# Ranking weight loads and splits ahead of their place in the recording, with new load durations, in a two-layer decoder trunk on one core

## The chip, the cores and the metric

The kernel runs on one core of one Trainium2 chip. Times are device microseconds (us) of one execution. TensorE is PE in the profile, VectorE is DVE, ScalarE is ACT, GpSimd is POOL, and SyncE is SP, whose queue issues the DMAs. PE's weight loads are a row of their own, PEld. TensorE's clock has two levels, 1.2 and 2.4 GHz; the profile gives the granted clock as a share of full speed (PEclk).

## The reference, cut to what matters

The input is one sequence of 512 tokens with 1024 features, and there are two layers (`DEPTH = 2`), each two half-step FFNs around a mixer with two branches:

```python
for l in range(DEPTH):
    x = x + 0.5 * swiglu(rmsnorm(x, ffn1_norm[l]), ffn1_w_gate_up[l], ffn1_w_down[l])
    h = rmsnorm(x, mix_norm[l])
    (q, kc, vc, ksel, vsel, kwin, vwin, g_nsa, uv, g_a, g_b) = \
        jnp.split(h @ w_in[l], IN_SPLITS, axis=-1)
    ...
    y_a = nsa_attention(...)
    y_b = spatial_gating(uv, sgu_norm[l], sgu_w_s[l], sgu_b_s[l])
    merged = jax.nn.sigmoid(g_a) * (y_a @ proj_a[l]) + jax.nn.sigmoid(g_b) * (y_b @ proj_b[l])
    x = x + merged @ w_out[l]
    x = x + 0.5 * swiglu(rmsnorm(x, ffn2_norm[l]), ffn2_w_gate_up[l], ffn2_w_down[l])
return rmsnorm(x, final_norm)
```

In `nsa_attention` the keys and values `kc` and `vc` are compressed: 31 overlapping windows of 32 tokens, plus a position term, go through a small network (`gelu(flat @ w1) @ w2`, called phi below). `spatial_gating` is `u * (tril(W_s) v + b)` on `gelu(uv)`, with `v` normalised. All weights are float32.

## The kernel before, in words

**Recording and ordering.** The kernel does not issue instructions as it runs. Every call on an engine goes through `Recorder.note`, which keeps the operation with the earlier operations it depends on, a rank, and a planned duration. The rank is the operation's index in the recording plus a bias of its engine (no bias is set for the engines here); the duration comes from `Recorder.cost`, as a pair: how long the engine is busy, and after how long the result can be used. `Recorder.order` is a list scheduler: again and again it takes the engine that can start earliest and, among the operations of that engine that are ready by then, the one with the lowest rank. `issue` emits the operations in the order found, so each engine, and SP's queue with its DMAs, runs them strictly in that order. All of them carry one line in the profile (L255, and L259 in the changed file).

**Weight tiles.** Nearly all the work of PE is 128-row tiles of weights against 512 tokens. `load` fetches one tile: SP copies 128x1024 float32 (512 KB) into `raw` (3 buffers), ACT copies it to `whi` (3 buffers, in the matmul format fp32r), and DVE computes `wlo = raw - whi` (2 buffers). The activations are split the same way, into `xh` and `xl` (`split`, `norm_operand`). `chain` then issues three matmuls for each of eight 128-row pieces: high by high, high by low, and low by high, 24 matmuls a tile. As `wlo` has two buffers, the subtraction for tile n overwrites what PE reads for tile n-2, and has to wait for it.

**The course of a layer.** `ffn` runs 44 gate and up tiles and three groups of eight down tiles. `mix` is the mixer. Its first part, in the order of recording:

- *Stage A:* projections of `kc` and `vc`; `windows` turns each into four tiles R18 to R21 (keys) or R14 to R17 (values): for each half of the partitions two DVE products (`t<-b,rbc`), one DVE sum (`t<-t,pes`) and a split into `R` on ACT and DVE. Then `proj_tok` with the weights wv (four banks b4 to b7), whose four steps are interleaved with the four of `phi` for keys (matmuls `b<-whi,R` and `b<-wlo,R`).
- *Stage B:* the gelu of that result into `YA`, a norm on it (`rsqrt`, then `YA<-YA,rv,ga` and the split into `VH` and `VL`, four each), while PE runs the `u` half (wu) and phi for values.
- *Stage C:* keys and queries with rotary tables (`roped`: ACT copies, DVE and POOL products, `R` splits and casts), the spatial gating (matmuls `b<-VH,whi`, then `U<-b,sgub,U`), transposes of `U` (`b<-cst,U`), and the first tiles of the gates (wB).

Then attention, the projections of both branches and wo follow, and the second `ffn`.

The program's first loads, before any matmul, are the gains, the eight pieces of `x`, and the first two weight tiles, on SP in turn; `norm_begin` and `norm_prep` make `xh`, `xl` and the squares of the norm.

Of the kernel before, what the change touches and what calls it, by code (L numbers as in the profile page):

```python
# [22 lines left out]
NG = (3 * DEPTH + 1) * KD  # L23
CHUNKS = ((0, 8), (8, 16), (16, 22))
LAG = 1
NEG = -1e30
EPS = 1e-6

# [10 lines left out]
class View:  # L39


    def __init__(self, buf, steps, ids, parts, dtype):
        self.buf, self.steps, self.ids, self.parts, self.dtype = buf, steps, ids, parts, dtype
        self.gen = buf.gen
# [88 lines left out]

class Recorder:
    def __init__(self, nc):
        self.nc, self.ops, self.rings, self.bias = nc, [], {}, {}
        self.real = {"PE": nc.tensor, "DVE": nc.vector, "ACT": nc.scalar, "POOL": nc.gpsimd, "SP": nc.sync}

    def ring(self, tag, n, cols, dtype=F32, psum=False):
# [19 lines left out]
    def note(self, engine, op, args, kw):  # L159
        outs = [v for v in [args[0], kw.get("accum_out")] if isinstance(v, View)]  # L160
        ins = [v for v in list(args[1:]) + [v for k, v in kw.items() if k != "accum_out"] if isinstance(v, View)]
        i, deps = len(self.ops), set()
        for v, writes in [(v, False) for v in ins] + [(v, True) for v in outs]:
            assert v.gen == v.buf.gen, v.buf.name
            q, e = v.region()
            keep = []
            for j, jw, jq, je in v.buf.log:
                if (writes or jw) and jq & q and je & e:
                    if j != i:
                        deps.add(j)  # L170
                    if writes and jq & ~q == 0 and je & ~e == 0:
                        continue
                keep.append((j, jw, jq, je))
            keep.append((i, writes, q, e))
            v.buf.log = keep
        self.ops.append((engine, op, args, kw, deps, i + self.bias.get(engine, 0), self.cost(engine, op, args, kw, outs, ins)))

    def cost(self, engine, op, args, kw, outs, ins):

        if engine == "PE":  # L180
            n = outs[0].ids.size
            if op == "transpose":
                return 109, 280
            rhs = kw["rhs"]
            if rhs.dtype == F32:
                t = 2 * max(109, n / 1.2 + 3)
                return t, t + 165
            t = max(109, n / 2.4 + 13.3)
            return t, t + 165
        if engine == "SP":  # L190
            v = outs[0] if outs else ins[0]
            size = (v.parts[1] - v.parts[0]) * v.ids.size * 4
            return 100 + size / 190, 2000 + size / 330
        a, b = SBUF_COST[engine]
        n = max(v.ids.size for v in outs + ins)
        if engine == "DVE" and op in ("tensor_copy", "tensor_scalar") and not any(v.buf.psum for v in ins):
            b = 0.52
        if op == "memset":
            b = b / 2
        t = a + b * n  # L200
        if kw.get("accum_out") is not None:
            t += 190 if engine == "ACT" else 83
        return t, t

    def order(self):
        ops = self.ops
        users, left = [[] for _ in ops], [len(o[4]) for o in ops]
        for i, o in enumerate(ops):
            for j in o[4]:
                users[j].append(i)  # L210
        ready = [0.0] * len(ops)
        free = dict.fromkeys(self.real, 0.0)
        cand = {e: [] for e in self.real}
        table, out = 0, []
        for i, o in enumerate(ops):
            if not left[i]:
                cand[o[0]].append(i)
        while len(out) < len(ops):
            best = None
            for e, c in cand.items():  # L220
                if not c:
                    continue
                t = max(free[e], min(ready[i] for i in c))
                if best is None or t < best[0]:
                    best = t, e
            t, e = best
            i = min((i for i in cand[e] if ready[i] <= t), key=lambda i: ops[i][5])
            cand[e].remove(i)
            busy, lat = ops[i][6]
            if e == "ACT":  # L230
                f = next((a for a in list(ops[i][2]) + list(ops[i][3].values()) if a in TABLES), None) \
                    if ops[i][1] == "activation" else None
                if f is not None and TABLES[f] != table:
                    table, busy, lat = TABLES[f], busy + 1283, lat + 1283
            free[e] = t + busy
            out.append(i)
            for u in users[i]:
                same = ops[u][0] == e
                ready[u] = max(ready[u], t + (busy if same and e != "SP" else lat + 70))
                left[u] -= 1  # L240
                if not left[u]:
                    cand[ops[u][0]].append(u)
        self.span = max(free.values())
        return out
# [14 lines left out]
def trunk(ctx: ExitStack, tc, d):  # L259
    rec = Recorder(tc.nc)  # L260
# [41 lines left out]
    def f(ap):  # L302
        return ap.bitcast(F32)

    def split(hi, lo, src):

        act(hi, src, AF.Copy)
        vec.tensor_tensor(lo, src, f(hi), op=ALU.subtract)
# [3 lines left out]
    def stage(src, n, mask=None):  # L312
        if first:
            return first.pop(0)
        return load(src, n, mask)

    def load(src, n, mask=None):
        raw, hi, lo = (rec.tile(t, [P, 1024]) for t in ("raw", "whi", "wlo"))
        sync.dma_start(raw[:, :n], src)
        if mask is not None:  # L320
            mask(raw)
        split(hi[:, :n], lo[:, :n], raw[:, :n])
        return hi, lo

    def mm3(ps, lh, ll, rh, rl, start, stop):
# [7 lines left out]
    def chain(ps, ops):  # L333

        n = len(ops)
        for k in range(n + LAG):
            if k < n:
                lh, _, rh, rl = ops[k]
                pe.matmul(ps, lhsT=lh, rhs=rh, start=k == 0, stop=False)
                pe.matmul(ps, lhsT=lh, rhs=rl, start=False, stop=False)  # L340
            if k >= LAG:
                _, ll, rh, _ = ops[k - LAG]
                pe.matmul(ps, lhsT=ll, rhs=rh, start=False, stop=k == n + LAG - 1)

# [601 lines left out]
    for k in range(KD):  # L946
        sync.dma_start(x[:, k, :], d["x"][k])
        if k < 2:
            first.append(load(d["gu1"][0, k], 1024))
# [16 lines left out]
def layout(inp):  # L966
# [60 lines left out]
    c[:, C_TRI:C_TRI + P] = r[:, None] <= r[None, :]  # L1027
    c[:, C_MASK + 384:C_MASK + 512] = np.where(r[None, :] <= r[:, None], 0.0, NEG)
    c[:, C_CM:C_CM + 56] = np.where(16 * (np.arange(56)[None, :] - 24) + 31 <= r[:, None], 0.0, NEG)
    c[:, C_VAL] = r >= 31  # L1030
# [24 lines left out]
```

## Time and profile before

| | |
|---|---|
| median of 3 runs | 2235.32 us (2233.21 to 2235.88) |
| the profiled execution | 2233.7 us, span of its instructions 2231.9 us |
| mean granted TensorE clock | 0.991 |
| busy: PE, PEld | 2187.2 us (98%), 1808.3 us (81%) |
| busy: DVE, ACT, POOL | 1158.8 us (52%), 889.9 us (40%), 258.4 us (12%) |
| DMA | 207.3 MB by SP's queue, mean 94 GB/s |
| a 512 KB load of gate/up weights | 3.5 us from issue to landing (median of 176) |
| all waits of PE: on DVE `wlo`, ACT `whi`, DVE `U`, DVE `VL` | 15.5, 11.1, 6.7, 2.5 us |

The profile is one execution. The busy time of an engine counts from the start to the modelled end of its instructions, and matmuls overlap, so a matmul's own duration is longer than its distance to the next. "Waits" are times in which an engine had nothing running, put down to what released it. A "window" is a stretch of the span with the busy time of each engine in it, and the granted clock averaged over it. PE waits for nothing from 30 to 370 us or from 600 to 1480 us: its waits lie in the first 24 us, in the first part of the mixer of each layer (stages A to C), and in the last 11 us.

### The profile page before, as it was taken

How to read it: one execution, taken by the hardware profiler on the slowest of the kernel's cores; microseconds unless marked ns; L12 is line 12 of the kernel's file. 1: busy time of each engine (PE TensorE's matmuls, PEld its weight loads, DVE VectorE, ACT ScalarE, POOL GpSimd, SP SyncE). 2: the span in 40 equal slices, each digit the busy share in tenths (PEclk: the TensorE clock that was granted, in tenths of full speed). 3: DMA queues.
4: the chain of work that ended last, by engine and by line, in shares of the span. 5: the costliest groups of instructions: out<-in, count | busy, mean ns of one | idle time of the engine just before them, and what ended most of it. 6: DMA issues, size and time to landing. Idle time of an engine off the chain costs nothing. (4 is left out here: it accounts for less than half of the span.)

```text
span 2231.9 us, 25665 instructions
## 1 busy us (share of the span) xinstructions
PE 2187.2 (98%) x10018; PEld 1808.3 (81%) x10018; DVE 1158.8 (52%) x1884; ACT 889.9 (40%) x1414; POOL 258.4 (12%) x165
## 2 busy tenths in 40 slices
PE   8999999889999999999999999999999999999998
PEld 6888888678888888888888888877788888888887
DVE  5334346568886433333543333374788855333334
ACT  5223234466663432322432232345666534323233
POOL 2102012010000120111211020110100001101011
PEclk9999999999999999999999999999999999999999
DMA  4323323322113233333333223234211233323322
GB/s 166 103 95 95 98 94 93 118 90 73 55 60 100 99 96 101 97 95 95 95 102 100 95 95 100 87 98 136 78 57 57 62 107 91 99 95 95 101 93 80
DMA packets 61033, 208.95 MB, mean 94 GB/s; under 512 B 7280, under 2 KB 7792, under 8 KB 60912
## 3 DMA queue, kind: packets, MB, share of 16 engines
q1 hardware_dynamic: 60912, 207.32, 29.6%
q8 instruction: 78, 1.28, 0.2%
q14 instruction: 43, 0.35, 0.0%
HBM read 205.19 MB, written 2.10 MB: 93 GB/s over the span
## 5 line engine op out<-in xcount | busy, mean ns | idle before, releaser
L255 ACT ACTIVATE whi<-raw 128x1024 fp32r<-128x1024 f32 (+2 forms) x396 | 409.0, 1036 | 904.1 <-PE b L255 855.5
L255 PE MATMUL b<-xh,whi 128*128 128x512 f32 x1920 | 754.0, 393 | 9.6 <-ACT whi L255 9.5
L255 PE MATMUL b<-xl,whi 128*128 128x512 f32 x1920 | 753.2, 392 | 0.3 <-DVE xl L255 0.3
L255 PE MATMUL b<-xh,wlo 128*128 128x512 f32 x1920 | 717.6, 393 | 1.6 <-DVE wlo L255 1.5
L255 DVE TENSOR_TENSOR wlo<-raw,whi 128x1024 fp32r<-128x1024 f32 (+2 forms) x396 | 471.2, 1191 | 88.8 <-PE b L255 56.6
L255 PEld LDWEIGHTS b<-xh,whi 128*128 128x128 f32 x1920 | 362.0, 189 | 86.5 <-ACT whi L255 11.5
L255 PEld LDWEIGHTS b<-xh,wlo 128*128 128x128 f32 x1920 | 361.6, 188 | 78.1 <-DVE wlo L255 3.6
L255 PEld LDWEIGHTS b<-xl,whi 128*128 128x128 f32 x1920 | 362.0, 189 | 76.0 <-DVE xl L255 1.7
L255 PE MATMUL b<-R,whi 128*128 128x512 f32 (+1 forms) x1428 | 420.1, 387 | 0.0
L255 DVE TENSOR_TENSOR t<-b,rbc 128x512 f32<-128x512 f32 (+1 forms) x192 | 132.4, 690 | 404.0 <-PE b L255 403.4
L255 POOL TENSOR_TENSOR t<-t,t 128x512 f32<-128x512 f32 x88 | 184.4, 2095 | 1153.0 <-DVE t L255 1143.2
L255 PEld LDWEIGHTS b<-R,whi 128*128 128x128 f32 x1428 | 267.1, 188 | 55.4
L255 PE MATMUL b<-R,wlo 128*128 128x512 f32 (+1 forms) x714 | 260.4, 387 | 0.0
L255 DVE SCALAR_TENSOR_TENSOR x<-b,x 128x512 f32<-128x512 f32 (+1 forms) x113 | 77.7, 687 | 296.4 <-PE b L255 296.4
L255 ACT ACTIVATE R<-t 128x512 fp32r<-128x512 f32 (+3 forms) x152 | 81.4, 551 | 242.2 <-POOL t L255 214.0
L255 DVE TENSOR_TENSOR R<-t,R 128x512 fp32r<-128x512 f32 (+3 forms) x152 | 91.7, 616 | 164.1 <-ACT R L255 163.5
L255 PEld LDWEIGHTS b<-R,wlo 128*128 128x128 f32 x714 | 134.0, 188 | 26.9
L255 PE MATMUL b<-R,R 128*128 128x512 f32 (+3 forms) x416 | 116.5, 358 | 0.2
L255 POOL TENSOR_TENSOR ga<-ga,t 128x512 f32<-128x512 f32 x35 | 48.7, 1391 | 419.5 <-ACT t L255 419.3
L255 PEld LDWEIGHTS b<-R,R 128*128 128x128 f32 x416 | 74.3, 189 | 13.0 <-DVE R L255 0.6
L255 ACT ACTIVATE R<-b 128x512 fp32r<-128x512 f32 (+1 forms) x84 | 48.3, 580 | 79.1 <-PE b L255 74.7
L255 PE MATMUL b<-wlo,xh 128*128 128x512 f32 (+1 forms) x192 | 72.4, 378 | 1.3 <-DVE wlo L255 1.3
(132 smaller groups left out, 1605.0 us busy)
## 6 DMA issues: line engine op xcount, KB each, us to landing
raw<-in_gu_dram SPq DMA_DIRECT2D x176, 512.0 KB, 3.5
raw<-in_dn_dram SPq DMA_DIRECT2D x64, 512.0 KB, 3.5
raw<-in_wA_dram SPq DMA_DIRECT2D x48, 512.0 KB, 3.5
raw<-in_dn_dram SPq DMA_DIRECT2D x32, 384.0 KB, 3.1
raw<-in_phi_dram SPq DMA_DIRECT2D x16, 512.0 KB, 4.0
raw<-in_wo_dram SPq DMA_DIRECT2D x16, 512.0 KB, 3.6
raw<-in_wv_dram SPq DMA_DIRECT2D x8, 512.0 KB, 3.8
raw<-in_wu_dram SPq DMA_DIRECT2D x8, 512.0 KB, 3.7
```

The source lines that it names most:

```text
L255: getattr(self.real[engine], op)(*args, **kw)
```

## The change

Two things change, both in the recorder. First, while `load` records its DMA, a mask if there is one, and the two operations of its split, their rank is lowered by `AHEAD = 100`, so that among ready operations of an engine they are taken before any other whose index is up to 100 lower. Second, the planned time of a DMA is new. Before, a transfer of `size` bytes kept SP busy for 100 + size/190 ns and was usable after 2000 + size/330 ns, each by itself (2859 and 3589 ns for 512 KB). Now it keeps SP busy for 430 ns, and the data of all transfers go through one pipe one after another, at 400 bytes per ns, after 2000 ns each (1311 ns of pipe for 512 KB).

```diff
+AHEAD = 100
...
-        self.nc, self.ops, self.rings, self.bias = nc, [], {}, {}
+        self.nc, self.ops, self.rings, self.bias, self.ahead = nc, [], {}, {}, 0
...
-        self.ops.append((engine, op, args, kw, deps, i + self.bias.get(engine, 0), self.cost(engine, op, args, kw, outs, ins)))
+        self.ops.append((engine, op, args, kw, deps, i + self.bias.get(engine, 0) - self.ahead, self.cost(engine, op, args, kw, outs, ins)))
...
-            return 100 + size / 190, 2000 + size / 330
+            return 430, size / 400
...
-        table, out = 0, []
+        table, out, dma = 0, [], 0.0
...
+            if e == "SP":
+                dma = max(dma, t + 2000) + lat
+                lat = dma - t
...
+        rec.ahead = AHEAD
         sync.dma_start(raw[:, :n], src)
         if mask is not None:
             mask(raw)
         split(hi[:, :n], lo[:, :n], raw[:, :n])
+        rec.ahead = 0
```

Every engine issues the same operations as before. POOL's order does not change. On SP little moves: at the start the loads of the first two weight tiles go ahead of the gains and all of `x`, and at the mixer's start the load of `pes` goes behind two further weight loads. ACT, DVE and PE change order in some hundreds of places, nearly all in the mixer; in the FFNs a `wlo` changes places with one neighbour. Three places follow, all on DVE in layer 1 (layer 2 has them too).

**Stage A, the windows of keys and values.** Names: `t` are scratch tiles, b0 and b1 the projections, R18 to R21 the keys' windows and R14 to R17 the values'. Before, the end of that run of operations:

```order
L255 TENSOR_TENSOR t_0_77<-b1_0_164,rbc_0_69 64x496
L255 TENSOR_TENSOR t_1_78<-t_0_77,pes_0_65 128x496
L255 TENSOR_TENSOR wlo_1_116<-raw_2_76,whi_2_114 128x1024
L255 TENSOR_TENSOR R14_0_137<-t_1_78,R14_0_137 128x4x31
L255 TENSOR_TENSOR R15_0_138<-t_1_78,R15_0_138 128x4x31
L255 TENSOR_TENSOR R16_0_139<-t_1_78,R16_0_139 128x4x31
L255 TENSOR_TENSOR R17_0_140<-t_1_78,R17_0_140 128x4x31
L255 TENSOR_TENSOR wlo_0_115<-raw_0_74,whi_0_112 128x1024
L255 TENSOR_TENSOR wlo_1_116<-raw_1_75,whi_1_113 128x1024
```

Now, the start of it:

```order
L259 TENSOR_TENSOR R18_0_141<-t_1_78,R18_0_141 128x4x31
L259 TENSOR_TENSOR wlo_1_116<-raw_2_76,whi_2_114 128x1024
L259 TENSOR_TENSOR R19_0_142<-t_1_78,R19_0_142 128x4x31
L259 TENSOR_TENSOR R20_0_143<-t_1_78,R20_0_143 128x4x31
L259 TENSOR_TENSOR R21_0_144<-t_1_78,R21_0_144 128x4x31
L259 TENSOR_TENSOR t_2_79<-b0_0_163,rbc_0_69 64x496
L259 TENSOR_TENSOR t_0_77<-t_2_79,pes_0_65 128x496
L259 TENSOR_TENSOR t_1_78<-b1_0_164,rbc_0_69 64x496
L259 TENSOR_TENSOR R18_0_141<-t_0_77,R18_0_141 128x4x31
```

The split `wlo_1` of phi's first tile stood behind the windows of the keys and nearly all of the values'; now it stands behind the first split into R18. The next splits, `wlo_0` and `wlo_1` of wv and phi, also move from the end of the run into its middle.

**Stage B, the norm of the gated half.** Names: `sm4`, `ss` and `rv` are the norm's small tiles, `YA` its operand, `VL` the low half. Before:

```order
L255 TENSOR_TENSOR wlo_1_116<-raw_0_74,whi_0_112 128x1024
L255 TENSOR_SCALAR sm4_6_106<-ss_0_98 128x4
L255 RECIPROCAL sm4_7_107<-sm4_0_100 128x4
L255 TENSOR_TENSOR sm4_0_100<-sm4_7_107 128x4
L255 TENSOR_TENSOR sm4_0_100<-sm4_0_100,sm4_6_106 128x4
L255 SCALAR_TENSOR_TENSOR rv_0_99<-sm4_0_100,sm4_7_107 128x4
L255 SCALAR_TENSOR_TENSOR YA_0_72<-YA_0_72,rv_0_99,ga_2_84 128x512 x4
L255 TENSOR_TENSOR VL_0_118<-YA_0_72,VH_0_117 128x512 x4
L255 TENSOR_TENSOR wlo_0_115<-raw_1_75,whi_1_113 128x1024
L255 TENSOR_TENSOR wlo_1_116<-raw_2_76,whi_2_114 128x1024
```

Now:

```order
L259 TENSOR_TENSOR wlo_1_116<-raw_0_74,whi_0_112 128x1024
L259 TENSOR_SCALAR sm4_6_106<-ss_0_98 128x4
L259 TENSOR_TENSOR wlo_0_115<-raw_1_75,whi_1_113 128x1024
L259 RECIPROCAL sm4_7_107<-sm4_0_100 128x4
L259 TENSOR_TENSOR sm4_0_100<-sm4_7_107 128x4
L259 TENSOR_TENSOR sm4_0_100<-sm4_0_100,sm4_6_106 128x4
L259 SCALAR_TENSOR_TENSOR rv_0_99<-sm4_0_100,sm4_7_107 128x4
L259 SCALAR_TENSOR_TENSOR YA_0_72<-YA_0_72,rv_0_99,ga_2_84 128x512
L259 TENSOR_TENSOR wlo_1_116<-raw_2_76,whi_2_114 128x1024
L259 SCALAR_TENSOR_TENSOR YA_0_72<-YA_0_72,rv_0_99,ga_2_84 128x512
L259 TENSOR_TENSOR VL_0_118<-YA_0_72,VH_0_117 128x512
L259 SCALAR_TENSOR_TENSOR YA_0_72<-YA_0_72,rv_0_99,ga_2_84 128x512 x2
```

The two splits that stood behind four `YA` and four `VL` operations now stand before the reciprocal and behind the first `YA`.

**Stage C, queries and spatial gating.** Names: `U` is the gated output, b5 to b7 the spatial banks, R0 to R5 the queries. Before:

```order
L255 SCALAR_TENSOR_TENSOR U_0_71<-b5_0_168,sgub_0_66,U_0_71 128x4x64
L255 SCALAR_TENSOR_TENSOR U_0_71<-b6_0_169,sgub_0_66,U_0_71 128x4x64
L255 TENSOR_TENSOR t_0_77<-t_0_77,t_2_79 128x512
L255 SCALAR_TENSOR_TENSOR U_0_71<-b7_0_170,sgub_0_66,U_0_71 128x4x64
L255 TENSOR_TENSOR VL_0_118<-b5_0_168,VH_0_117 128x512
L255 TENSOR_TENSOR R1_0_124<-t_0_77,R1_0_124 64x512
L255 TENSOR_TENSOR R5_0_128<-t_0_77,R5_0_128 64x512
L255 TENSOR_TENSOR VL_0_118<-b6_0_169,VH_0_117 128x512
L255 TENSOR_TENSOR VL_0_118<-b7_0_170,VH_0_117 128x512
L255 TENSOR_TENSOR VL_0_118<-b5_0_168,VH_0_117 128x512
L255 TENSOR_TENSOR wlo_1_116<-raw_0_74,whi_0_112 128x1024
L255 TENSOR_TENSOR wlo_0_115<-raw_1_75,whi_1_113 128x1024
```

Now, from an earlier point of the same stretch:

```order
L259 TENSOR_TENSOR t_1_78<-t_1_78,t_0_77 128x512
L259 TENSOR_TENSOR wlo_1_116<-raw_0_74,whi_0_112 128x1024
L259 TENSOR_TENSOR R0_0_123<-t_1_78,R0_0_123 64x512
L259 TENSOR_TENSOR R4_0_127<-t_1_78,R4_0_127 64x512
L259 TENSOR_TENSOR t_0_77<-b1_0_164,ga_3_85 128x512
L259 SCALAR_TENSOR_TENSOR U_0_71<-b6_0_169,sgub_0_66,U_0_71 128x4x64
L259 SCALAR_TENSOR_TENSOR U_0_71<-b7_0_170,sgub_0_66,U_0_71 128x4x64
L259 SCALAR_TENSOR_TENSOR U_0_71<-b5_0_168,sgub_0_66,U_0_71 128x4x64
L259 TENSOR_TENSOR t_0_77<-t_0_77,t_2_79 128x512
L259 SCALAR_TENSOR_TENSOR U_0_71<-b6_0_169,sgub_0_66,U_0_71 128x4x64
L259 SCALAR_TENSOR_TENSOR U_0_71<-b7_0_170,sgub_0_66,U_0_71 128x4x64
L259 TENSOR_TENSOR R1_0_124<-t_0_77,R1_0_124 64x512
```

The split of a query's weights moves ahead of a query's `R` operations and of the `U` run; in PE's order that query's matmuls move up among the spatial ones, too.

## Rows read from the trace of the kernel before

**Rows 1.** The page, section 1: busy us (share of the span) and instructions of PE.

```profile
PE 2187.2 (98%) x10018; PEld 1808.3 (81%) x10018; DVE 1158.8 (52%) x1884; ACT 889.9 (40%) x1414; POOL 258.4 (12%) x165
```

**Rows 2.** Waits of PE from 370 to 412 us: releaser: us in total, times, longest.

```profile
PE b L255 <- DVE wlo L255: 4.9, 2, 4.1
```

**Rows 3.** Waits of PE from 412 to 456 us.

```profile
PE b L255 <- DVE wlo L255: 2.5, 2, 2.2
PE b L255 <- ACT whi L255: 1.5, 2, 0.8
```

**Rows 4.** Waits of PE from 456 to 500 us.

```profile
PE b L255 <- DVE U L255: 3.3, 2, 1.9
PE b L255 <- DVE VL L255: 1.1, 3, 0.7
PE b L255 <- DVE wlo L255: 0.7, 1, 0.7
```

**Rows 5.** Waits of PE from 1480 to 1602 us, the same place in layer 2.

```profile
PE b L255 <- DVE wlo L255: 7.4, 4, 4.2
PE b L255 <- DVE U L255: 3.4, 2, 1.9
PE b L255 <- ACT whi L255: 1.6, 2, 0.8
PE b L255 <- DVE VL L255: 1.3, 3, 0.9
```

**Rows 6.** Windows: length, PE, PEld, DVE, ACT, POOL busy (x), PEclk, DMA share, GB/s.

```profile
370.00:412.00 42.00, 37.13 (x160) 30.01 (x159) 28.26 (x49) 14.49 (x29) 3.58 (x10) 0.92 0.30 92
412.00:456.00 44.00, 39.91 (x189) 31.82 (x187) 21.95 (x34) 28.93 (x47) 0.00 (x0) 0.96 0.44 137
456.00:500.00 44.00, 38.73 (x175) 31.55 (x174) 33.46 (x48) 28.47 (x49) 5.60 (x4) 0.92 0.23 73
1480.00:1514.00 34.00, 29.85 (x130) 24.24 (x129) 24.11 (x44) 11.05 (x24) 2.55 (x2) 0.90 0.30 94
1514.00:1558.00 44.00, 39.86 (x193) 31.81 (x192) 21.95 (x34) 28.92 (x47) 0.00 (x0) 1.00 0.44 138
1558.00:1602.00 44.00, 38.48 (x174) 31.07 (x174) 32.78 (x48) 27.87 (x48) 5.69 (x4) 0.92 0.24 74
397.50:404.30 6.80, 6.08 (x15) 4.75 (x15) 1.88 (x2) 1.06 (x1) 0.00 (x0) 0.50 0.73 225
```

**Rows 7.** Timeline of PE, 394.5 to 440 us: start, us, what, [idle before <-releaser].

```profile
396.37 0.39 PE L255 MATMUL b<-wlo,R 128*128 128x256 f32 x1 [4.15 <-DVE wlo L255]
...
399.32 0.63 PE L255 MATMUL b<-whi,xh 128*128 128x512 f32 x1
399.74 0.63 PE L255 MATMUL b<-wlo,xh 128*128 128x512 f32 x1
...
434.43 1.09 PE L255 MATMUL b<-whi,xh 128*128 128x512 f32 x4
```

**Rows 8.** Timeline of DVE: two places where the split that PE waited for ended.

```profile
395.09 1.22 DVE L255 TENSOR_TENSOR wlo<-raw,whi 128x1024 fp32r<-128x1024 f32 x1
...
436.45 2.35 DVE L255 TENSOR_TENSOR wlo<-raw,whi 128x1024 fp32r<-128x1024 f32 x2
```

**Rows 9.** Timeline of PE, the first 26 us.

```profile
6.48 0.80 PE L255 MATMUL b<-xh,whi 128*128 128x512 f32 x1 [6.48 <-ACT whi L255]
...
23.51 0.50 PE L255 MATMUL b<-xh,whi 128*128 128x512 f32 x1 [1.50 <-ACT whi L255]
```

**Rows 10.** Window of the head, columns as in rows 6.

```profile
2.50:15.00 12.50, 8.24 (x25) 5.79 (x26) 8.21 (x8) 10.20 (x17) 5.80 (x4) 1.00 1.00 372
```

**Rows 11.** Timelines of DVE and POOL: a sum beside a POOL operation.

```profile
468.91 0.68 DVE L255 TENSOR_TENSOR R<-t,R 64x512 fp32r<-64x512 f32 x1
...
470.50 1.70 DVE L255 TENSOR_TENSOR R<-t,R 64x512 fp32r<-64x512 f32 x1
...
470.34 1.30 POOL L255 TENSOR_TENSOR t<-t,ga 128x512 f32<-128x512 f32 x1 [5.50 <-ACT t L255]
```

## The prediction

> **What bounds the kernel now.** I read first the busy time of the page, then the waits of PE, stage by stage, then windows with the granted clock, and last the timelines of PE and DVE where PE waits. The busy time says that PE is the bound: 2187.2 us, 98% [rows 1]; DVE, ACT and POOL have room as a share of the whole. So what a change of order can win is what PE stands still, and what it runs at half clock. The waits show where it stands still. In the first part of the mixer of layer 1, PE waits 4.9 us in stage A, all of it for DVE's `wlo` [rows 2], 4.0 us in stage B for `wlo` and `whi` [rows 3], and 5.1 us in stage C for `U`, `VL` and `wlo` [rows 4]: 14.0 us. Layer 2 repeats it with 13.7 us [rows 5], so both mixers hold 27.7 us. The head has 6.48 us before the first matmul and 1.50 us before the third tile [rows 9]. The FFNs have nothing to give.
>
> The clock is the second thing to see. The waits are followed by stretches at a granted clock of 0.50, 1.2 GHz, as from 397.50 to 404.30 [rows 6], where matmuls of 512 columns start 0.42 us apart, while four at full clock fit into 1.09 us with the last one's tail [rows 7]. From the mean clocks, (1 - clock) x length x 2: 6.7, 3.5, 7.0, 6.8, 0 and 7.0 us [rows 6], together 31.0 us at half clock. These matmuls count as busy, so the 98% hides them; half of 31.0, 15.5 us, is lost time.
>
> The Trainium skill, page Perfetto Trace Analysis, section Identifying the Most-Contended Engine, says that matmul busy share does not show how near PE is to its limit, and that the busy share of weight loads is better. By that, 81% would leave several hundred us of room. The rows speak for its first half (the half clock is hidden) and against so much room, as outside the mixers PE waits for nothing.
>
> What PE waits for is not late data: in stage A the split it needed began at 395.09 on DVE and took 1.22 us, right up to the matmul at 396.37 that had waited 4.15 us [rows 7, 8]. By the order of before, the split stood behind nearly all the operations of the two windows. In stage B two splits began at 436.45 [rows 8], behind four `YA` and four `VL`.
>
> **The change, part by part.** No instruction is added or removed, so the sum has only moved waits.
>
> *New durations of loads.* They are the scheduler's picture and cost nothing by themselves. As loads rank first and SP's order hardly moves beyond the head, I put them at 0; SP waits for a free buffer nearly always, and the next load is issued as soon as one is. The load of `pes` that now goes out behind two more loads is that of the next layer, not needed for half the program; 0.
>
> *Stage A.* `wlo_1` comes directly after the first split into R18, at about 387, so the first phi matmuls wait only for the second half of R18 and the 4.15 us go. Three splits of 1.22 us now stand ahead of windows operations, and the norm's column products come a little later, so the windows end later. Walking the new orders of DVE and PE with the old durations, I find three small waits left, 0.8, 0.5 and 0.5 us, with rounding 1.85 a layer. Saved 4.9 - 1.85 = 3.05 in layer 1; in layer 2, where stage A has 4.2 of the 7.4 us of `wlo` [rows 5], 2.35.
>
> *Stage B.* The two splits are now before the reciprocal and behind the first `YA`, over 4 us earlier than 436.45 (four `VL` and three `YA` now follow, at some 0.68 each, an estimate from a DVE sum of 512 columns [rows 11]), and the 2.2 us wait shrinks to nothing but what ACT's `whi` and PE's own order bring: phi's matmuls of the values move ahead of six of wu's, which uncovers about 0.6 twice. I leave 2.25 of 4.0 and save 1.75; in layer 2 (4.1: 2.5 as in layer 1, and `whi` 1.6) 1.85.
>
> *Stage C.* A query's split moves ahead of the `R` and `U` operations, and its 24 matmuls fill what were waits for `U`. But by my walk with the old durations the DVE sum ahead of the split ends at about 480.3, the split 1.22 later, at 481.5, and PE, without its old waits, wants it at 479.2: 2.35 left, and 0.55 at the gates. Saved 5.1 - 2.9 = 2.2; in layer 2 (3.4 + 1.3 + 0.7 = 5.4) 2.5. Here a rule could hit: beside a POOL sum that began at 470.34, a DVE sum took 1.70 us instead of 0.68 [rows 11]. The new place of the split lies behind the DVE sum that reads POOL's result, so POOL is then idle, and I take 1.22.
>
> The Trainium skill, page SBUF — State Buffer, section Who interferes with whom, says that a DVE instruction with two SBUF inputs shuts out a GpSimd one that reads SBUF, or is shut out by it, for its whole length. The `wlo` subtraction is such a one. By it, one hit in each stage C would cost about 1 us a layer, and the sum would be 2 us smaller.
>
> *Clock.* With the waits cut from 27.7 to 14.0 and spread out, fewer stretches should fall to half clock. I take two of 3.4 us left in each layer, 13.6 of 31.0 us, and save 17.4 / 2 = 8.7. The ends are 0 and 15.5.
>
> *Head.* Two weight tiles now go ahead of `x`, so 512 KB more arrive before the first matmul can start: at 372 GB/s [rows 10] 1.4 us, of which 0.3 comes back as `xh` (an ACT copy of half the size) and not `whi` is then last: first matmul at about 7.6. In return DVE makes all `xl` before the squares' sums run on POOL, worth about 1.0 for the one `xl` on the path (a DVE sum was 1.0 shorter without POOL beside it [rows 11]), and `whi` of the third tile precedes most of the squares, so the 1.50 [rows 9] goes. Net gain 1.50 + 1.0 - 1.1 = 1.4; the ends are -1.5 (the wait stays) and +3.
>
> *FFNs.* A `wlo` now stands ahead of the product `t` or `x` of the tile before. Both wait for the same end of a tile on PE, so the product is 1.22 us later, covered by the next tile's 24 matmuls, over 5 us at four in about 1 us [rows 7]. Where the next step needs `xl` of the last tile, at the five borders between FFNs and mixers, the cover is thinnest; if it went there, 5 x 1.22 = 6.1 us. I take 0.
>
> **The sum.** Stages 3.05 + 2.35 + 1.75 + 1.85 + 2.2 + 2.5 = 13.7, clock 8.7, head 1.4: 23.8 us off the profiled execution's 2233.7, so 2209.9. The median of the runs is 1.6 above that execution, so I forecast 2212.
>
> **The rivals.**
>
> *Waits only move.* DVE is busy 33.46 of 44 us in stage C and 28.26 of 42 in stage A [rows 6], nearly without a gap where PE waits. A split taken early makes `R`, `YA`, `U` late by as much, and PE waits for those. Against it: in stage A the values' windows, which are put off, are needed only in stage B. If it holds in all stages, only the head's -1.5 to +3 is left, about 2233 on the median's scale.
>
> *The clock does not come back.* The waits shrink but are still many, and each falls among short matmuls. For it: both stages C stand at 0.92 with no wait over 1.9 us [rows 4 to 6]; against it: from 1514 to 1558 the same waits as in layer 1's stage B left the clock at 1.00 [rows 6]. Then 13.7 + 1.4 = 15.1 are saved: 2220. The Trainium skill, page TensorE: Matmul & The Clock Gate, section A second HAM failure mode: psum-queue depth-cycling, tells of such a case: short idling between groups of matmuls keeps the clock going up and down. It would give this same time; no run here shows it yet.
>
> *Slower: a split ranked first blocks its engine.* An engine takes its operations in order, so a `wlo` or `whi` that must wait for PE to leave its buffer holds whatever is behind it. Six `wlo` a layer now stand ahead of windows, norm or spatial work in stages A to C, twelve in all. If PE needs what is held, it stops. It eats the 23.8 us from 2.0 us a piece on, and shows as slower beyond 2.4; at half a tile, 2.7 us, 12 x 2.7 = 32.4 against 23.8 gives +8.6, so 2244. Against it: in most of these places the buffer is free about when the split is reached, by my walk.
>
> *The change does nothing of what it says.* If the loads' new durations were the point, nothing would come: transfers are not what PE waits for. The order shows the splits moved, so this has no chance of its own.
>
> **How the numbers follow.** A measurement of this kernel can tell 0.2%, about 4.5 us, from no change. Forecast 0.62; clock not back 0.18; waits only move 0.12; slower 0.08. The first two are faster, 0.80; the third is the same; the fourth slower. Range: at the low end half of the remaining 14.0 us goes too, with all of the clock: 13.7 + 7 + 15.5 + 1.4 = 37.6, so 2198. At the high end only stage A's 5.4 us come, with half of the 6.75 us that its 13.5 us at half clock lose, 3.4, less 1.5 in the head: 7.3, so 2228.
>
> **What would show it.** Right: waits of PE from 370 to 500 us near 7 instead of 14.0, stage A's first phi matmul without a wait over 1 us, the mean clock at 0.95 or more in each stage, the third tile starting near 21 to 22 without a wait. Wrong: waits for `R`, `YA` or `U` in the place of those for `wlo`; clocks of 0.92 as before; a wait on ACT or DVE that itself waits for PE; a FFN with waits at its borders; a first matmul after 9 us.

## The result and the profile after

| | before | after |
|---|---|---|
| median of 4 runs | 2235.38 us | 2200.98 us (2200.54 to 2203.23) |
| profiled execution | 2233.7 us, span 2231.9 | 2200.54 us, span 2198.7 |
| mean granted clock | 0.991 | 0.997 |

The ratio is 0.985, with a 95% interval of 0.9833 to 0.9867: 34.4 us less by the medians. 2212 was forecast, a gain of 23 us; the time lies inside the range, 3 us above its low end. The four executions before lie high: the 40 beside the experiments below have medians of 2232.9 to 2233.2 us, and from 2233.16 the gain is 32.2 us.

The page's busy time of the changed kernel, and its clock by slices:

```profile
PE 2172.7 (99%) x10018; PEld 1797.2 (82%) x10018; DVE 1153.1 (52%) x1884; ACT 886.9 (40%) x1414; POOL 185.6 (8%) x165
...
PEclk9999999999999999999999999999999999999999
```

PE is busy 14.5 us less with the same 10018 matmuls [rows 1]; the rest of the 33.2 us of span is idle time that is gone. The waits of PE, from 370 to 411, 412 to 456 and 456 to 500 us (stages A, B and C of layer 1), then from 1460 to 1602 us (all three of layer 2); the rows of before are [rows 2] to [rows 5]:

```profile
PE b L259 <- DVE R L259: 0.6, 1, 0.6
PE b L259 <- DVE ga L259: 0.4, 1, 0.4
...
PE b L259 <- ACT whi L259: 0.8, 3, 0.4
PE b L259 <- DVE wlo L259: 0.7, 2, 0.4
...
PE b L259 <- DVE wlo L259: 2.2, 1, 2.2
...
PE b L259 <- DVE wlo L259: 2.9, 3, 2.2
PE b L259 <- ACT whi L259: 1.0, 3, 0.4
PE b L259 <- DVE R L259: 0.6, 1, 0.6
PE b L259 <- DVE ga L259: 0.4, 1, 0.4
```

Stage A keeps 1.0 of 4.9 us (a further 0.1 for `wlo` is too short for a row of its own), stage B 1.5 of 4.0, stage C 2.2 of 5.1, layer 2 4.9 of 13.7. The wait of 4.15 us at phi's first matmul is gone, and nothing of its size came elsewhere. Of 27.7 us of waits in the mixers 9.7 are left. The split that began at 395.09 [rows 8] now begins 9.2 us earlier (DVE's row first, then PE's two for phi's start):

```profile
385.86 1.22 DVE L259 TENSOR_TENSOR wlo<-raw,whi 128x1024 fp32r<-128x1024 f32 x1
...
390.45 0.36 PE L259 MATMUL b<-whi,R 128*128 128x256 f32 x1 [0.59 <-DVE R L259]
390.64 0.28 PE L259 MATMUL b<-wlo,R 128*128 128x256 f32 x1
```

The windows of the same stages, columns as in [rows 6]:

```profile
370.00:412.00 42.00, 40.71 (x192) 32.75 (x191) 30.45 (x52) 20.17 (x37) 3.16 (x7) 1.00 0.41 119
412.00:456.00 44.00, 42.70 (x205) 34.01 (x205) 26.22 (x39) 32.77 (x61) 1.30 (x1) 1.00 0.48 145
456.00:500.00 44.00, 41.76 (x240) 36.38 (x239) 38.70 (x62) 32.65 (x56) 7.15 (x5) 0.96 0.30 89
1465.00:1500.00 35.00, 34.31 (x161) 27.71 (x161) 25.78 (x45) 15.23 (x31) 2.54 (x2) 1.00 0.35 109
1500.00:1544.00 44.00, 42.26 (x204) 33.63 (x203) 25.57 (x38) 32.18 (x60) 1.30 (x1) 1.00 0.47 147
1544.00:1588.00 44.00, 41.77 (x245) 36.24 (x244) 39.60 (x64) 33.71 (x58) 7.15 (x5) 1.00 0.29 88
```

The granted clock is 1.00 in five of six; 0.96 in a window of 44 us is one stretch of 3.4 us at half clock. Before, there were 31 us of it. So the 33.2 us come apart as follows: 27.7 - 9.7 = 18.0 us of waits; (31.0 - 3.5) / 2 = 13.8 us of clock; and about 1.9 us in the head, as the 401st matmul of the trace starts at 100.24 instead of 102.17. That makes 33.7. A new wait of 0.4 us for the squares' sum `ga` at 1102, between the layers, goes off; two more like it are in the rows above.

The sum closes better than its parts. The 1601st, 1771st, 1916th and 2146th matmul of the trace (6591st, 6761st, 6906th and 7136th in layer 2) bound the three stages in both kernels, as PE has issued the same work up to each. Between them stage A takes 11.0 us less in the two layers together, B 5.7 and C 15.2, while waits and half of the time at half clock, counted between the same matmuls, say 13.7, 5.8 and 12.4. So for a single stage this way of counting is off by up to 3 us, and what makes the difference stays open.

The head, in the timeline of PE:

```profile
7.59 1.22 PE L259 MATMUL b<-xh,whi 128*128 128x512 f32 x2 [7.59 <-ACT xh L259]
...
20.80 0.39 PE L259 MATMUL b<-xh,whi 128*128 128x512 f32 x1
...
25.34 0.95 PE L259 MATMUL b<-ones,ga 128*128 128x1 f32 x8
```

The first matmul starts at 7.59 (before 6.48) and the third tile at 20.80 (before 23.51, after a wait of 1.50 [rows 9]); its column products for the norm stand behind that tile now, at 25.34, and not ahead of it.

### The profile page after: what moved, and what is told of

The parts are those of the page before. It is cut to its first block, busy times and chain, and to the rows that moved or that the text cites. A ratio compares the mean times of both kernels' runs of the same rounds, so it can differ in the third digit from the quotient of the medians.

```text
span 2198.7 us, 25769 instructions
## 1 busy us (share of the span) xinstructions
PE 2172.7 (99%) x10018; PEld 1797.2 (82%) x10018; DVE 1153.1 (52%) x1884; ACT 886.9 (40%) x1414; POOL 185.6 (8%) x165
## 4 chain that ended last, share of the span: by engine, by line
PE 93%; DVE 4%; issue 1%; DMA 1%; ACT 1%; SPq 0%; DVEq 0%; ACTq 0%
PE b L259 93%; DVE wlo L259 1%; DVE t L259 1%; DVE R L259 1%; DMA raw<-in_phi_dram 0%; ACT whi L259 0%; DMA x<-in_x_dram 0%; ACT t L259 0%; DVE x L259 0%; DVE xl L259 0%; DVE YA L259 0%; DVE ga L259 0%; DVE U L259 0%; SPq L259 0%; DVE rbc L259 0%
## 5 line engine op out<-in xcount | busy, mean ns | idle before, releaser
L259 ACT ACTIVATE whi<-raw 128x1024 fp32r<-128x1024 f32 (+3 forms) x396 | 409.7, 1036 | 719.3 <-PE b L259 700.1
L259 POOL TENSOR_TENSOR t<-t,t 128x512 f32<-128x512 f32 x88 | 113.7, 1292 | 1214.6 <-DVE t L259 1202.5
L259 ACT ACTIVATE t<-t 128x512 f32<-128x512 f32 (+1 forms) x92 | 57.4, 623 | 115.3 <-DVE t L259 115.3
```

Of the source, the lines that this page charges most:

```text
L259: getattr(self.real[engine], op)(*args, **kw)
```

## The experiments

All twelve runs are edits of the changed kernel. Times are medians; a ratio is to the kernel before, with its interval, which had a median of 2232.9 to 2233.2 us beside them.

**Durations alone.**

```diff
-AHEAD = 100
+AHEAD = 0
```

> The new load durations with AHEAD = 0. Theory (the rank brings it all): the splits in the mixer stand where they stood before, so PE waits some 27 us in the two mixers as before and the time is 2232 to 2237 us. Rival (the scheduler's truer picture of loads brings a good part): splits move forward by themselves and the time falls below 2220 us.

Measured: 2230.45 us, ratio 0.9987 (0.9977 to 0.9996). The theory holds in the mixers, where PE and DVE have the order of before and PE waits 27.7 us, as before. But the time is 2.7 us below before, 1.5 us under the range that was expected, and this comes from the head: the 401st matmul starts at 99.71, 2.5 us earlier than before. ACT's timeline shows why:

```profile
12.94 1.66 ACT L259 ACTIVATE t<-x 128x512 f32<-128x512 f32 x3
14.91 1.06 ACT L259 ACTIVATE whi<-raw 128x1024 fp32r<-128x1024 f32 x1 [0.31 <-DMA raw<-in_gu_dram]
```

ACT makes the `whi` of the third tile as soon as its load has landed, at 14.91, among the squares. The scheduler with the old durations believed the load to come later. PE's waits in the first 30 us are then only the one of 6.5 us to the first matmul and two small ones for `xl`; the wait of 1.50 [rows 9] is gone.

**Rank alone.**

```diff
-            return 430, size / 400
+            return 100 + size / 190, 2000 + size / 330
...
-            if e == "SP":
-                dma = max(dma, t + 2000) + lat
-                lat = dma - t
```

> AHEAD = 100 with the load durations of before. Theory: DVE's order in the mixers is that of the change, so the waits there are about 10 us and the time is that of the change but for the head, where the squares stand between the xh copies again: 2200 to 2205 us. Rival (durations matter): above 2215 us.

Measured: 2201.23 us, ratio 0.9854 (0.9839 to 0.9869). The rank carries the mixers. In the head it gives nothing by itself: the 401st matmul starts at 104.03, 1.9 us later than before, of which 1.7 are a stretch of 3.4 us at half clock that begins at 24.7. The first matmul starts 1.5 us later, and the wait of 1.50 us is there again, in front of the third tile,

```profile
PE b L256 <- ACT xh L256: 8.0, 1, 8.0
PE b L256 <- ACT whi L256: 1.5, 1, 1.5
```

because `whi` is back behind the square root of the norm on ACT:

```profile
22.48 0.26 ACT L256 ACTIVATE sm<-b,eps 128x4 f32<-128x4 f32 x1 [4.39 <-DVE sm L256]
22.64 2.00 ACT L256 ACTIVATE whi<-raw 128x1024 fp32r<-128x1024 f32 x2
```

It is as fast as the change because its stage C happens to come out better: a wait of 1.6 us instead of 2.2, and no drop of the clock.

**Only the DMA ranked ahead.**

```diff
         rec.ahead = AHEAD
         sync.dma_start(raw[:, :n], src)
+        rec.ahead = 0
         if mask is not None:
             mask(raw)
         split(hi[:, :n], lo[:, :n], raw[:, :n])
-        rec.ahead = 0
```

> Only the load's DMA is ranked ahead, not its split; new durations. Theory (late splits, not late data): 2231 to 2237 us, with the waits of before in the mixers. Rival (an earlier load is what counts): below 2220 us.

Measured: 2231.67 us, ratio 0.9992 (0.9983 to 1.0002): no gain beyond the head's, with the waits of 4.15 and 2.21 us in both layers. Late data was not what PE waited for.

**Only wlo ranked ahead.**

```diff
-        rec.ahead = AHEAD
         sync.dma_start(raw[:, :n], src)
         if mask is not None:
             mask(raw)
-        split(hi[:, :n], lo[:, :n], raw[:, :n])
+        act(hi[:, :n], raw[:, :n], AF.Copy)
+        rec.ahead = AHEAD
+        vec.tensor_tensor(lo[:, :n], raw[:, :n], f(hi[:, :n]), op=ALU.subtract)
         rec.ahead = 0
```

> Only the subtraction wlo on DVE is ranked ahead, not the DMA and not ACT's copy whi; new durations. Theory: DVE's order is what PE waited for, ACT's moves little, so most of the gain is there without the head's: 2202 to 2212 us, with waits for whi of 3 us as in before. Rival (ACT's copies ranked ahead carry half): 2215 to 2222 us.

Measured: 2202.57 us, ratio 0.9863 (0.9848 to 0.9877). One operation per tile, the subtraction on DVE, brings nearly all of it; the waits for `whi` of 0.8 us, two a layer, 3.1 us in all, are there as expected.

**One stage at a time.** `st["part"]` is set to "F" in `ffn`, and in `mix` to "A", "B", "C" and, behind stage C, "R"; the rank is lowered in one part alone ("F" and "R" together in the last).

```diff
-        rec.ahead = AHEAD
+        rec.ahead = AHEAD if st.get("part", "F") in "A" else 0
```

> The rank is lowered only for loads recorded in stage A (kc, vc projections, wv, phi of keys). If each stage keeps what its waits and its clock gave: waits there from 9.1 to about 2.2 us in the two layers, 6.9 us, and 13.7 us of half clock gone, 6.8 us: 2235.4 - 13.7 = 2221.7 us. Rival (a wait removed in one stage comes back in the next): the waits of stage B or C grow by 3 us or more a layer and the time stays above 2228 us.

> The rank is lowered only for loads recorded in stage B (wu, phi of values). By the terms: waits there from 8.1 to about 3.2 us, 4.9, and one stretch of 3.4 us at half clock gone, 1.7: 2228.8 us. Rival (waits move on): no gain, above 2233 us.

> The rank is lowered only for loads recorded in stage C (keys, queries, spatial, wB). By the terms: waits there from 10.5 to about 4.4 us, 6.1, and 10.2 us of half clock gone, 5.1: 2224.2 us. Rival (waits move on): above 2231 us.

> The rank is lowered only for loads recorded in the FFNs, the head included, and behind stage C (attention, projections). By the terms only the head's 2 us are here: 2233.4 us. Rival one (the FFNs and the attention give as well, not seen as waits): below 2229 us. Rival two (a split ranked first blocks its engine in the FFNs): above 2237 us.

| ranked ahead in | median, us | ratio (interval) | below durations alone, 2230.45 |
|---|---|---|---|
| A | 2220.01 | 0.9940 (0.9923 to 0.9956) | 10.4 |
| B | 2225.46 | 0.9967 (0.9954 to 0.9980) | 5.0 |
| C | 2215.50 | 0.9919 (0.9904 to 0.9934) | 15.0 |
| the rest | 2231.20 | 0.9990 (0.9981 to 1.0000) | -0.8 |

All four have the new durations, so the last column is what a part's rank gives. The sum is 29.6; the whole change gives 2230.45 - 2200.98 = 29.5. The runs of one version differ by 2 to 3 us, so that close a match is luck, but within some 3 us the stages add up, and what is removed in one does not come back in the next. Each stage alone also gives about what it gives within the change (11.0, 5.7 and 15.2 us by the matmuls above). The expectations, which counted from 2235.4, had 13.7 for A, 6.6 for B and 11.2 for C: A and B gave less, C more. PE's waits with stage A alone, from 370 to 405, 412 to 449 and 449 to 500 us, which are stages A, B and C of layer 1 there:

```profile
PE b L259 <- DVE R L259: 0.6, 1, 0.6
...
PE b L259 <- DVE wlo L259: 2.5, 2, 2.2
PE b L259 <- ACT whi L259: 1.5, 2, 0.8
...
PE b L259 <- DVE U L259: 3.4, 2, 1.9
PE b L259 <- DVE VL L259: 1.6, 3, 1.1
PE b L259 <- DVE wlo L259: 0.7, 1, 0.7
```

A's 4.9 are 0.7 with a wait of 0.1 too short for a row, and B and C keep theirs, 4.0 and 5.7. Stage C alone, in the same three windows:

```profile
PE b L259 <- DVE wlo L259: 4.1, 1, 4.1
...
PE b L259 <- DVE wlo L259: 2.5, 2, 2.2
PE b L259 <- ACT whi L259: 0.8, 1, 0.8
...
PE b L259 <- DVE wlo L259: 2.2, 1, 2.2
PE b L259 <- ACT whi L259: 0.2, 1, 0.2
```

Here A keeps its 4.1, B its 2.5 and one `whi` of 0.8, and C has 2.4. The second `whi` wait of 0.8, that of C's first load, had been counted to stage B; it is 0.2 here, which moves 0.6 us a layer from B's term to C's. C gave 15.0 where 11.2 was expected, in part because the durations alone have more to lose there than the kernel before: in their trace, stage C waits 6.0 and 5.6 us, against 2.2 twice here, and has 13.7 us at half clock against 3.4. That is 7.1 + 1.2 + 5.1 = 13.4; the other 1.6 us show neither as waits nor as clock.

**AHEAD = 200.**

```diff
-AHEAD = 100
+AHEAD = 200
```

> AHEAD = 200 everywhere. In the order of the mixers the query's split of stage C stands three operations earlier; in the head a third weight tile is loaded and copied before the first xh. Theory (rank too far blocks the engine in order): the head loses about 1.5 us (first matmul near 9.2 instead of 7.6), stage C's wait of 2.2 us falls below 1.0 us in each layer, so 2198 to 2201 us. Rival (a rank further ahead blocks in the mixers as well): waits there above 12 us and more than 2204 us.

Measured: 2204.49 us, ratio 0.987 (0.9854 to 0.9887), 3.5 us slower than the change. The head loses, but less than expected at its start, 8.67:

```profile
8.67 0.79 PE L259 MATMUL b<-xh,whi 128*128 128x512 f32 x1 [8.67 <-ACT xh L259]
...
392.91 0.50 PE L259 MATMUL b<-wlo,xh 128*128 128x512 f32 x1 [1.55 <-DVE wlo L259]
```

ACT's timeline shows the blocking: three `whi`, each behind its load, before the first `xh`, though the first piece of `x` (256 KB) would take only some 0.7 us of transfer, an estimate at the 372 GB/s of [rows 10]:

```profile
4.33 1.06 ACT L259 ACTIVATE whi<-raw 128x1024 fp32r<-128x1024 f32 x1 [2.10 <-DMA raw<-in_gu_dram]
5.59 1.06 ACT L259 ACTIVATE whi<-raw 128x1024 fp32r<-128x1024 f32 x1 [0.21 <-DMA raw<-in_gu_dram]
6.95 1.06 ACT L259 ACTIVATE whi<-raw 128x1024 fp32r<-128x1024 f32 x1 [0.30 <-DMA raw<-in_gu_dram]
7.91 4.69 ACT L259 ACTIVATE xh<-x,gains 128x512 fp32r<-128x512 f32 x7
```

In stage A a wait of 1.55 us stands where the change has 0.1 and 0.6, stage C's wait is 1.8 and not below 1.0, and two new ones of 0.3 and 0.55 follow it. The mixers' waits are 12.8 us, so here the rival is right: a rank further ahead blocks in the mixers as well.

**AHEAD = 200 or 100 in the mixer's stages, 0 elsewhere.**

```diff
-        rec.ahead = AHEAD
+        rec.ahead = {"F": 0, "R": 0, "A": 200, "B": 200, "C": 200}[st.get("part", "F")]
```

> AHEAD = 200 in stages A to C of the mixer alone, 0 elsewhere. Theory (the gain is the sum of the mixers' stages and of the head's new durations, the rank in the head costs): stage C's wait falls below 1.0 us, the head is that of durations_alone, 0.5 us better than the change's: 2195 to 2198.5 us. Rival (AHEAD = 100 had all there is): 2200 us or more.

> AHEAD = 100 in stages A to C of the mixer alone, 0 elsewhere. Theory (the rank gives nothing in FFNs, attention and head): 2199.5 to 2201.5 us, no slower than the change. Rival (the ranking of the FFNs' splits holds waits away): 2203 us or more.

Measured: 2201.19 us (ratio 0.9853, 0.9839 to 0.9868) and 2200.64 us (0.9852, 0.9837 to 0.9867). The second theory holds: the rank in the FFNs, the attention and the head gives nothing. The first falls: stage C's wait is 1.8 and stage A's 1.5, the mixers' waits are 11.8 us against 9.1 with 100, and only a clock without any drop there (two with 100, 3.4 us) makes up for it. Neither version is faster than the change. The 3.3 us between AHEAD = 200 with and without the rest are, by the traces, 1.1 us of the head (401st matmul at 100.86 and 99.78), 1.2 us of three waits for `ga`, and one stretch of half clock, 1.7; by the spans it is 4.4 us.

**AHEAD = 40.**

> AHEAD = 40 everywhere: in the order stage B stands as before, stage A's first phi split is only two operations earlier, stage C's query split is ahead of the U run. Theory (each stage gives what its own splits gain in place): stage C's 12 to 15 us and 3 us in stage A come, B's 5 do not: 2213 to 2219 us. Rival (the waits removed in C come back elsewhere): above 2224 us.

Its edit is `AHEAD = 40`. Measured: 2222.46 us, ratio 0.9951 (0.9936 to 0.9966): slower than the theory's range, below the rival's. B stands as before (2.2 us), as it should. A's wait of 4.15 is split in two, 2.46 and 1.66, and gives nothing: the first subtraction is earlier, but the next one is late, and the stretch at half clock stays. C gives about 8 us and not 12 to 15, as the waits for `U` (2.1 and 1.4 us) stay; those for `VL` go. So a stage's term needs the whole of its splits moved far enough, which the theory had not seen.

## Why the prediction was right, and where it was short

**What bounds the kernel, right.** PE waited for splits that stood behind other work on DVE. Two runs show it from both sides: ranking only the DMA gives nothing beyond the head, ranking only `wlo` gives all but 1.6 us. PE's own order changes along with DVE's wherever there is a gain, and no run holds it fixed. In stage A the trace settles that it is not PE's: before, PE was ready for phi's first `wlo` at 392.2, and it takes it at 390.6 now, earlier by hardly less than the 1.9 us of the head, while the split is 9.2 us earlier. For B and C the two orders are not told apart.

**Stage A, right, 3.05 + 2.35 forecast.** The waits left are 1.1 us and not 1.85; with its clock it is worth 10.4 us alone.

**Stage B, right, 1.75 + 1.85 forecast.** 1.5 us are left of 4.0 instead of 2.25; 5.0 us alone. The new small waits from PE's own order were 0.2 to 0.4, not 0.6 twice.

**Stage C, right in mechanism.** The residue that the prediction named, a query's split that comes 2.35 us late, is there with 2.21:

```profile
469.75 0.80 PE L259 MATMUL b<-xh,wlo 128*128 128x512 f32 x1 [2.21 <-DVE wlo L259]
```

DVE's timeline shows where that split stood, 468.48, and a sum before it:

```profile
462.07 1.78 DVE L259 TENSOR_TENSOR t<-t,t 128x512 f32<-128x512 f32 x1
...
468.48 1.22 DVE L259 TENSOR_TENSOR wlo<-raw,whi 128x1024 fp32r<-128x1024 f32 x1
```

ACT's, with POOL's row beside it, what its `whi` stood behind:

```profile
463.89 1.29 ACT L259 ACTIVATE R<-t 64x512 fp32r<-64x512 f32 x2 [1.95 <-DVE t L259]
465.21 1.06 ACT L259 ACTIVATE whi<-raw 128x1024 fp32r<-128x1024 f32 x1
...
462.02 1.29 POOL L259 TENSOR_TENSOR t<-t,ga 128x512 f32<-128x512 f32 x1 [2.56 <-ACT t L259]
```

The copy `whi` stands on ACT behind two `R` copies that wait for a sum on DVE, which took 1.78 us beside POOL's product (1.29 us from 462.02) instead of 0.68; the split on DVE then stands behind the next query's casts. So the contention that the prediction weighed does exist in this stage, one step ahead of the place where it looked for it; up to 1.1 us of the 2.21 may come from there, but no run takes it out. The 0.55 at the gates that was to remain did not.

**Clock: the term that was mis-sized.** Forecast were four stretches of 3.4 us left, 8.7 us saved; one is left, 13.8 saved. (The four runs have mean clocks of 0.996 to 0.998, so the profiled one with 0.997 is no exception.) That is 5.1 of the 9.4 us by which the sum of 23.8 was short of the 33.2 measured; the waits (18.0 for 13.7) are 4.3, the head 0.5, less the new 0.4 at 1102. The rival that the clock does not come back fell with it.

**New durations, wrong.** They were put at 0; alone they are worth 2.7 us, and it is they that bring the third tile's `whi` forward, which the prediction gave to the rank. The seven traces with PE's head order of the durations alone have the 401st matmul between 99.71 and 100.97, the five with the rank in the head as well (of the DMA at least) between 100.24 and 100.86, before at 102.17. So the head's term of 1.4 (1.9 measured; first matmul forecast at 7.6, measured at 7.59) had about the right sum with a wrong cause, which is luck.

**FFNs, right.** Nothing gained or lost beyond the three waits of 0.4 us: 2231.20 with the rank there alone, against 2230.45 without.

**The other rivals.** That waits only move fell with the stages that add up to the whole. That a split ranked first blocks its engine is real, but small: with AHEAD = 200 it is 1.1 us more to the first matmul and 1.55 us in stage A, and 3.5 us in all.

## What to carry to other kernels

Where the bound engine waits, look at what stood in front of the operation that released it, on that operation's own queue: here a subtraction of 1.22 us was held 4 us behind work that nobody needed yet, and moving that one operation per tile gave 30.6 of 32.2 us. Count the clock with each wait: a wait of 4 us cost another 1.7 to 3.4 us at half clock, so over the whole kernel such waits were worth about half as much again as they show; for a single stage that count was off by up to 3 us. And test a planner's costs apart from its priorities: here the costs moved the program's start and the priorities the mixers.

## What the runs showed of the hardware that was not expected

**The clock falls after some waits of the same length and not after others.** In the traces of all these runs, each wait of 4.15 us (12 of them) has a stretch at clock 0.50 that begins in it or within 1.2 us behind it. Of 20 waits of 2.2 us 12 have one, often in one layer and not in the other, as at 469.75 in the changed kernel but not at its twin 1558.8. After the six waits of 1.5 to 1.6 us in the mixers of rank alone and of the two kernels with 200, there was none, but the wait of 1.50 us in the head of rank alone has one, where the same wait before [rows 9] has none. What decides is not shown. The spread of the runs goes along with it: of the kernel before, the executions with a mean clock of 0.990 took 2235.3 to 2238.0 us, those with 0.993 took 2230.6 to 2231.3 us, and 0.003 of 2232 us is 6.7 us.

**POOL's product in the FFNs fell from 2.10 to 1.29 us.** The group's row of before:

```profile
L255 POOL TENSOR_TENSOR t<-t,t 128x512 f32<-128x512 f32 x88 | 184.4, 2095 | 1153.0 <-DVE t L255 1143.2 <-ACT t L255 9.8
```

of the changed kernel:

```profile
L259 POOL TENSOR_TENSOR t<-t,t 128x512 f32<-128x512 f32 x88 | 113.7, 1292 | 1214.6 <-DVE t L259 1202.5 <-ACT t L259 12.0
```

and of the mixer alone with 100, where the FFNs stand in the order of before:

```profile
L259 POOL TENSOR_TENSOR t<-t,t 128x512 f32<-128x512 f32 x88 | 183.1, 2080 | 1149.2 <-DVE t L259 1138.3 <-ACT t L259 10.9
```

Before, the split ran beside the product (DVE's row first, then POOL's):

```profile
101.62 1.22 DVE L255 TENSOR_TENSOR wlo<-raw,whi 128x1024 fp32r<-128x1024 f32 x1
...
101.84 2.14 POOL L255 TENSOR_TENSOR t<-t,t 128x512 f32<-128x512 f32 x1 [8.74 <-DVE t L255]
```

In the changed kernel the split precedes the product's factor, and POOL runs alone:

```profile
99.13 1.23 DVE L259 TENSOR_TENSOR wlo<-raw,whi 128x1024 fp32r<-128x1024 f32 x1 [3.67 <-issue]
100.28 0.69 DVE L259 TENSOR_TENSOR t<-b,rbc 128x512 f32<-128x512 f32 x1
...
101.11 1.28 POOL L259 TENSOR_TENSOR t<-t,t 128x512 f32<-128x512 f32 x1 [9.60 <-DVE t L259]
```

The Trainium skill, page SBUF — State Buffer, section Who interferes with whom, says that a DVE instruction with two SBUF inputs and a GpSimd one that reads SBUF exclude each other; the 0.8 us more beside a split that had 1.0 us to go when the product began agree with that, as does the sum of 1.78 us beside a product of 1.29 us in stage C. It is some 70 us of POOL's time, and worth nothing here: the mixer alone with 100 has the slow product and the same time as the change.
